# Three down projections as seven products of quadrants for eight, with the sums of quadrants on POOL

## Chip, cores, metric

One of the eight cores of one Trainium2 chip. The metric is the device time of one execution in microseconds, the median over runs.

## The reference

Two transformer blocks of different make over 512 tokens of width 1024; everything is float32. Block one (depth 1) ends with a feed-forward stage of width 4096, block two (depth 2) has in each layer a gated feed-forward stage of width 2816 with a causal convolution over three tokens. Cut to these:

```python
# block one
h2 = rmsnorm(x, norm_ffn_g[l])
x = x + jnp.square(jax.nn.relu(h2 @ w_ff1[l])) @ w_ff2[l]
# block two, in each of two layers
up = u @ w_up
a, g = up[..., :D_FF_2], up[..., D_FF_2:]
a = causal_depthwise_conv(a, conv_w, conv_b)
return (jax.nn.gelu(a, approximate=False) * g) @ w_down
```

`w_ff2` (4096 x 1024) and the two `w_down` (2816 x 1024) are the three down projections.

## The kernel before

Activations lie with features on the 128 partitions and the 512 tokens as columns: `self.x[m]` is feature block m of 8. To keep float32 precision each operand is split into a rounded part and its remainder (`wh`, `wl` for weights, `x.h`, `x.l` for activations) and each product is three matmuls of 512 columns, all three in `lin` (line 503): `wh` x `x.h`, `wl` x `x.h`, `wh` x `x.l`. All matmuls are issued at line 379 (`mm`), all DVE, ACT and POOL instructions at line 221 (a wrapper).

Weights come in chunks of up to 128 x 1024. `fill` (line 426) keeps three chunks in flight on SP's queue (line 432, tile `raw`). ACT copies a chunk into `wh` with rounding (`whi`, line 436), DVE subtracts (`wlo`, line 451) into `wl`. There are four `wh` and three `wl` tiles; `nextw` (line 469) prepares chunks ahead, each time the projection before it has been issued.

`proj` (line 515) runs one output block: takes a PSUM tile, issues the matmuls of its chunks, then spawns its evacuation. In block one (`ffn1`, line 1461) a half of the hidden width is 16 up projections, each evacuated by `hid` (DVE multiplies by the row norm, squares after a comparison with zero, `split` at line 597 makes the two operands with ACT and DVE), then 8 down projections of 16 blocks, added into `self.x[m]` by `xadd` (line 1453). In block two (`ffn2`, line 1813) hidden block m takes two up projections: `conv` (DVE, ACT, DVE twice, ACT for the Gelu) and `gate` (DVE twice, then `split`); 16 blocks, then the down projection over them, then 6 blocks and theirs. In the last part each finished `x[m]` feeds the next norm (`fin1` at line 1502, `feed` at line 610: ACT, DVE, and squares added up on POOL by `sqadd`, line 627).

The order of the instructions on each engine is set when the program is built: generators (the stream of projections, the evacuations) are stepped by `drive` (line 301) in the order of an estimated time. Each engine then takes its own queue strictly in that order, and waits by semaphores.

## Time and profile before

| | |
|---|---|
| median of 3 runs | 2324.68 us (2323.86 to 2325.26) |
| the profiled execution, its own time | 2324.91 us |
| its span, first to last instruction | 2323.2 us |
| mean granted TensorE clock | 0.994 |
| PE, DVE, ACT, POOL busy | 98%, 65%, 46%, 21% of the span |

PE is the matmul engine, DVE the vector engine, ACT the scalar engine, POOL GpSimd, SP the queue that starts transfers. A busy share is an average over stages; which engine holds the others up is told by the waits and by the chain that ended last. Matmuls are pipelined: a row's duration is longer than the distance to the next start, and the distance is what counts in a row of matmuls. "L379" is a line of the kernel before.

### The profile page before, as it was taken

What the parts mean: (1) busy time and instruction counts of PE and PEld (TensorE: products, weight loads), DVE (VectorE), ACT (ScalarE), POOL (GpSimd) and SP (SyncE); (2) the same over time, 40 slices, a digit from 0 to 9 for tenths busy, and PEclk for the clock granted to TensorE, in tenths of its full rate; (3) what the DMA queues carried; (4) which work ended last, traced back from release to release, by engine and by line L of the source; (5) the groups of instructions that cost most, each with busy time, mean ns of one, the idle gap of its engine ahead of it and who ended that gap; (6) DMA issues with size and microseconds to landing.
All of it is one profiled execution on the core that took longest, in us unless ns stands there. A gap on an engine that the chain in (4) does not pass through costs nothing.

```text
span 2323.2 us, 29048 instructions
## 1 busy us (share of the span) xinstructions
PE 2278.9 (98%) x10810; PEld 1868.2 (80%) x10810; DVE 1518.4 (65%) x2375; ACT 1067.4 (46%) x1695; POOL 479.0 (21%) x571
## 2 busy tenths in 40 slices
PE   9999999999999999999999999999999999999998
PEld 6887877778888888887878888888887878888887
DVE  6878499976542554679975652457688866652466
ACT  4767466664322233466643331245556544332343
POOL 3523044431000002334430000002425320000012
PEclk9999999999999999999999999999999999999999
DMA  5321322123332222433333233323432332233332
GB/s 178 87 74 55 91 73 64 56 87 116 98 100 97 94 100 84 155 95 101 119 105 100 93 98 100 102 91 115 125 108 90 118 109 92 99 100 93 107 95 69
DMA packets 75727, 228.24 MB, mean 98 GB/s; under 512 B 9664, under 2 KB 15680, under 8 KB 75584
## 3 DMA queue, kind: packets, MB, share of 16 engines
q1 hardware_dynamic: 70400, 209.62, 28.2%
q0 software_dynamic: 5184, 16.75, 2.5%
q8 instruction: 85, 1.39, 0.3%
q14 instruction: 58, 0.48, 0.1%
HBM read 215.29 MB, written 6.32 MB: 95 GB/s over the span
## 4 chain that ended last, share of the span: by engine, by line
PE 87%; DVE 8%; issue 2%; POOL 1%; ACT 1%; DMA 0%; SPq 0%; POOLq 0%; DVEq 0%; ACTq 0%
PE lin L379 73%; PE v L379 5%; PE sc L379 3%; PE po L379 3%; DVE wl L221 2%; PE pt L389 2%; DVE xl L221 1%; DVE dg L221 1%; DVE eq L221 0%; DVE ks L221 0%; DVE pre L221 0%; DVE qk L221 0%; DVE ql L221 0%; DVE sl L221 0%; DVE suf L221 0%
## 5 line engine op out<-in xcount | busy, mean ns | idle before, releaser
L379 PE MATMUL lin<-xh,wh 128*128 128x512 f32 (+1 forms) x2752 | 1088.0, 395 | 0.0
L379 PE MATMUL lin<-xl,wh 128*128 128x512 f32 (+1 forms) x2752 | 1072.3, 390 | 6.7 <-DVE xl L221 6.7
L379 PE MATMUL lin<-xh,wl 128*128 128x512 f32 (+1 forms) x2728 | 1061.5, 389 | 0.0
L221 DVE TENSOR_TENSOR wl<-raw,wh 128x1024 fp32r<-128x1024 f32 (+3 forms) x391 | 468.9, 1199 | 500.8 <-PE lin L379 329.3
L221 ACT ACTIVATE wh<-raw 128x1024 fp32r<-128x1024 f32 (+4 forms) x394 | 392.4, 996 | 807.7 <-PE lin L379 659.8
L379 PEld LDWEIGHTS lin<-xl,wh 128*128 128x128 f32 x2752 | 517.3, 188 | 117.8 <-DVE xl L221 8.8
L379 PEld LDWEIGHTS lin<-xh,wh 128*128 128x128 f32 x2752 | 518.0, 188 | 105.0 <-issue 3.5
L379 PEld LDWEIGHTS lin<-xh,wl 128*128 128x128 f32 x2728 | 514.4, 189 | 96.7
L221 POOL TENSOR_TENSOR sq<-sq 128x512 f32<-128x512 f32 (+1 forms) x61 | 90.1, 1477 | 566.6 <-ACT sq L221 565.9
L221 POOL MEMSET pad<- 128x2 f32 x44 | 4.4, 99 | 586.3 <-DVE cv L221 586.3
L221 POOL TENSOR_SCALAR P<-P,r 128x128 f32<-128x128 f32 (+3 forms) x128 | 86.5, 681 | 149.3 <-DVE r L221 133.0
L221 DVE SCALAR_TENSOR_TENSOR cv<-pad,vec,cv 128x512 f32<-128x512 f32 x88 | 66.1, 752 | 40.7 <-ACT cv L221 39.0
L379 PE MATMUL v<-wh,xh 128*128 128x512 f32 x192 | 78.3, 408 | 0.7 <-POOL wh L221 0.7
L379 PE MATMUL v<-wl,xh 128*128 128x512 f32 x192 | 75.9, 395 | 3.1 <-DVE wl L221 3.1
L379 PE MATMUL v<-wh,xl 128*128 128x512 f32 x192 | 75.7, 394 | 0.0
L221 ACT ACTIVATE ph<-pt 128x512 fp32r<-128x512 f32 (+3 forms) x128 | 55.6, 435 | 42.2 <-PE pt L389 40.8
L221 DVE TENSOR_TENSOR x<-lin,x 128x512 f32<-128x512 f32 x80 | 54.6, 683 | 23.5 <-PE lin L379 23.5
L221 DVE TENSOR_TENSOR pl<-pt,ph 128x512 fp32r<-128x512 f32 (+3 forms) x128 | 60.2, 479 | 12.7 <-ACT ph L221 12.2
L221 ACT ACT_TABLE_LOAD x51 | 65.4, 1283 | 4.2 <-DVE qk L221 1.6
L221 ACT ACTIVATE P<-lg,m 128x128 f32<-128x128 f32 (+1 forms) x96 | 53.6, 558 | 28.9 <-DVE m L221 21.9
L221 ACT ACTIVATE tl<-po 64x512 f32<-64x512 f32 x56 | 33.2, 592 | 73.1 <-PE po L379 72.6
L221 DVE CUSTOM_DVE_ANT_0 lg<-sc,E 128x128 f32<-128x128 f32 (+1 forms) x96 | 45.6, 483 | 31.9 <-PE sc L379 23.1
(244 smaller groups left out, 2578.1 us busy)
## 6 DMA issues: line engine op xcount, KB each, us to landing
raw<-wup SPq DMA_DIRECT2D x88, 512.0 KB, 3.3
raw<-w SPq DMA_DIRECT2D x83, 512.0 KB, 3.6
raw<-wf SPq DMA_DIRECT2D x64, 512.0 KB, 3.3
raw<-wdn SPq DMA_DIRECT2D x32, 512.0 KB, 3.5
raw<-wv SPq DMA_DIRECT2D x22, 512.0 KB, 3.6
raw<-wpg SPq DMA_DIRECT2D x16, 512.0 KB, 3.3
raw<-wbr SPq DMA_DIRECT2D x12, 512.0 KB, 3.3
raw<-wdn SPq DMA_DIRECT2D x16, 384.0 KB, 3.1
```

What stands on the lines that cost most here:

```text
L221: r = f(*a, **k)
L379: self.nc.tensor.matmul(out, l, r, start=start, stop=stop)
L389: self.nc.tensor.transpose(out, src, self.ident)
```

## The change

Each down projection is cut into blocks of 256 x 256 weights by 256 x 512 activations, as 2 x 2 quadrants on both sides, and the eight quadrant products become seven (Strassen's algorithm in Winograd's form). The inner width goes in parts of four pairs of 128 (block two's last part has three): four parts in block one, three in each layer. `wino` makes two output blocks per call (a quad of weights): seven products, each 3 matmuls of 256 columns for every pair, into three PSUM tiles `wa`, `wg`, `we`; DVE adds partial results straight into the two blocks of `x`, seven additions. Product 3 goes on in the columns that product 0 wrote and its addition has read, product 4 in those of product 1, product 6 in those of 3.

On the weights' side POOL makes four sums of 512 columns per quad (`sums` and `wlo`), in place in the two raw chunks and in a `ws` tile; ACT and DVE then split seven operands. The third sum overwrites the quadrant that the first operand was split from. On the activations' side `hid` and `gate` now write a pair of hidden blocks into one tile, POOL makes four sums of 256 columns per pair and ACT and DVE split seven operands (`bops`). The product of the convolution's result with the row norm, which DVE did from PSUM on the gate, goes to POOL. Squaring goes to ACT. `canhi` and `canlo` prepare weights as soon as a tile's holder has been issued.

```diff
+def _quads(w, pairs):
+    k, m = w.shape
+    assert k == 256 * pairs
+    t = w.reshape(pairs, 2, 128, m // 256, 2, 128).transpose(3, 4, 2, 1, 0, 5)
+    return np.ascontiguousarray(t).reshape(m // 256, 2, 128, 256 * pairs)
...
-    o["wf2"] = _fm(A["w_ff2"][0])
+    o["wf2"] = np.stack([_quads(A["w_ff2"][0][1024 * q:1024 * q + 1024], 4) for q in range(4)])
...
-    o["wdn"] = np.stack([_fm(A["w_down_2"][i], 22)[:, 0] for i in range(2)])
+    o["wdn"] = np.stack([np.stack([_quads(A["w_down_2"][i][1024 * q:1024 * q + 1024], 4) for q in range(2)]) for i in range(2)])
+    o["wdl"] = np.stack([_quads(A["w_down_2"][i][2048:], 3) for i in range(2)])
...
+    def quad(self, ap, n):
+        q = Quad(128 * n, len(self.rawq))
+        for r in range(2):
+            self.rawq.append((ap[r], 256 * n))
+        for k in range(7):
+            self.wq.append((None, 128 * n, 0, q.raw + 1, q, k))
+    def room(self, tag, i):
+        o, n = self.own[tag], self.SLOTS[tag]
+        return len(o) < n or o[-n] < i
+    def canhi(self, i):
+        j = self.wsh
+        q, k = self.wq[j][4:6]
+        if self.wq[j][3] >= self.wdma:
+            return False
+        return self.room("wl" if q and k % 2 else "wh", i)
...
+        if q:
+            src = self.sums(q, k)
+            tag = "wl" if k % 2 else "wh"
+            t = self.ws.tile([128, 2 * cols], F32R, tag=tag, name=tag, bufs=self.SLOTS[tag])
+            self.own[tag].append(j)
+            self.ac.activation(t[:, 0:cols], src, AF.Copy)
+            self.wh[j], self.wl[j] = t[:, 0:cols], t[:, cols:2 * cols]
+            return
...
+    def sums(self, q, k):
+        n = q.n
+        if k == 0:
+            a, b = q.a, q.b = self.raw[q.raw], self.raw[q.raw + 1]
+            assert self.live["tri"] < self.cap["tri"]
+            self.live["tri"] += 1
+            q.t = self.trip.tile([128, 1280], F32, tag="tri", name="ws")
+            self.tags[id(q.t)] = ("tri", q.t)
+            self.pl.tensor_tensor(out=q.t[:, 0:n], in0=b[:, 0:n], in1=b[:, n:2 * n], op=ALU.add)
+            self.pl.tensor_tensor(out=b[:, 0:n], in0=a[:, 0:n], in1=b[:, 0:n], op=ALU.subtract)
+        return (q.a[:, 0:n], q.t[:, 0:n], q.a[:, n:2 * n], q.a[:, 0:n], q.t[:, 512:512 + n], q.b[:, n:2 * n], q.b[:, 0:n])[k]
...
+        if q:
+            self.dv.tensor_tensor(out=self.wl[j], in0=self.sums(q, k) if k else q.a[:, 0:q.n], in1=self.wh[j].bitcast(F32),
+                                  op=ALU.subtract)
+            n = q.n
+            if k == 0:
+                self.pl.tensor_tensor(out=q.a[:, 0:n], in0=q.t[:, 0:n], in1=q.a[:, 0:n], op=ALU.subtract)
+                self.pl.tensor_tensor(out=q.t[:, 512:512 + n], in0=q.a[:, n:2 * n], in1=q.a[:, 0:n], op=ALU.subtract)
+            if k == 4:
+                self.free(q.t)
+                self.raw.pop(q.raw)
+                self.rawdone += 1
+                self.fill()
+            if k == 6:
+                self.raw.pop(q.raw + 1)
+                self.rawdone += 1
+                self.fill()
+            return
...
-        while self.wsh < min(n, i + 4):
+        while self.wsh < n and self.canhi(i):
             self.whi()
-            while self.wsl < min(self.wsh - 1, i + 3):
+            while self.wsl < self.wsh - 1 and self.canlo(i):
                 self.wlo()
-        while self.wsl < min(n, i + 3, self.wsh):
+        while self.wsl < self.wsh and self.canlo(i):
             self.wlo()
...
+    def bops(self, pr):
+        h = S // 2
+        b11, b12, b21, b22 = (pr.t[:, h * j:h * j + h] for j in range(4))
+        def split(k, src):
+            o = pr.ops[k]
+            o.h = yield from self.g("bo", F32R)
+            self.ac.activation(o.h[:, 0:h], src, AF.Copy)
+            yield self.w("ac")
+            self.dv.tensor_tensor(out=o.h[:, h:S], in0=src, in1=o.h[:, 0:h].bitcast(F32), op=ALU.subtract)
+            self.sig(o.ev, "dv")
+        yield pr.e[0]
+        yield from self.take("tw", 1, 3)
+        T = yield from self.tri("T")
+        t1, t2, t3, t4 = (T[:, h * j:h * j + h] for j in range(4))
+        self.pl.tensor_tensor(out=t1, in0=b12, in1=b11, op=ALU.subtract)
+        yield from split(0, b11)
+        yield from split(1, t1)
+        yield pr.e[1]
+        self.pl.tensor_tensor(out=t2, in0=b22, in1=t1, op=ALU.subtract)
+        self.pl.tensor_tensor(out=t4, in0=b21, in1=t2, op=ALU.subtract)
+        self.pl.tensor_tensor(out=t3, in0=b22, in1=b12, op=ALU.subtract)
+        yield from split(2, b21)
+        yield from split(4, b22)
+        yield from split(3, t2)
+        yield from split(5, t4)
+        yield from split(6, t3)
+        yield self.w("dv")
+        self.free(pr.t, T)
+        self.give("tw", 2)
+    def btile(self, pr):
+        if pr.t is None:
+            yield from self.take("tw", 1, 3)
+            pr.t = yield from self.tri("bt")
+            self.spawn(self.bops(pr), 1)
+    def wino(self, ap, n, prs, m, done):
+        self.quad(ap, n)
+        h = S // 2
+        def run():
+            x1, x2 = self.x[m], self.x[m + 1]
+            def prod(k, o, start):
+                wh, wl = self.nextw()
+                for i in range(n):
+                    b = prs()[i].ops[k]
+                    yield from self.need(b)
+                    c = slice(128 * i, 128 * i + 128)
+                    self.mm(o, wh[:, c], b.h[:, 0:h], start and i == 0, False, True)
+                    self.mm(o, wl[:, c], b.h[:, 0:h], False, False, True)
+                    self.mm(o, wh[:, c], b.h[:, h:S], False, i == n - 1, True)
+                    yield None
+            def add(x, p):
+                self.dv.tensor_tensor(out=x, in0=p, in1=x, op=ALU.add)
+            a = yield from self.psr("lin", self.lincap, "wa")
+            yield from prod(0, a[:, 0:h], True)
+            add(x1[:, 0:h], a[:, 0:h])
+            g = yield from self.psr("lin", self.lincap, "wg")
+            yield from prod(1, g[:, 0:h], True)
+            add(x2[:, h:S], g[:, 0:h])
+            e = yield from self.psr("lin", self.lincap, "we")
+            yield from prod(2, e[:, 0:h], True)
+            yield from prod(3, a[:, 0:h], False)
+            add(x1[:, h:S], a[:, 0:h])
+            yield from prod(4, g[:, 0:h], False)
+            add(x1[:, h:S], g[:, 0:h])
+            self.free(g)
+            yield from prod(5, e[:, h:S], False)
+            add(x1[:, 0:h], e[:, 0:h])
+            add(x2[:, 0:h], e[:, h:S])
+            self.free(e)
+            yield from prod(6, a[:, 0:h], False)
+            u = a[:, 0:h]
+            add(x2.rearrange("p (a c) -> p a c", a=2), bass.AP(u.tensor, u.offset, [list(u.ap[0]), [0, 2], [1, h]]))
+            self.free(a)
+            if done:
+                for j in range(2):
+                    self.spawn(self.later(done, m + j), 0)
+        self.tasks.append(run)
...
-        def hid(X_):
+        def hid(pr, e):
             def run(ps):
-                nc = self.nc
-                t = yield from self.g("h")
+                yield from self.btile(pr)
+                t = pr.t[:, S * e:S * e + S]
                 yield N2.ev
-                self.dve_mul(t, ps, N2.rb)
+                self.dv.scalar_tensor_tensor(out=t, in0=ps, scalar=0.0, in1=N2.rb, op0=ALU.max, op1=ALU.mult)
                 self.free(ps)
-                self.dv.scalar_tensor_tensor(out=t, in0=t, scalar=0.0, in1=t, op0=ALU.max, op1=ALU.mult)
                 yield self.w("dv")
-                yield from self.split(t, X_)
+                self.ac.activation(t, t, AF.Square)
+                self.sig(pr.e[e], "ac")
             return run
 
         N = Norm()
         N1 = Norm()
-        for half in range(2):
-            hs = [X() for _ in range(16)]
-            for m in range(16):
-                self.proj([(I["wf1"][16 * half + m], 1024)], lambda: N2.xs, hid(hs[m]))
-            if half:
+        for part in range(4):
+            prs = [Pair() for _ in range(4)]
+            for m in range(8):
+                self.proj([(I["wf1"][8 * part + m], 1024)], lambda: N2.xs, hid(prs[m // 2], m % 2))
+            if part == 3:
                 self.call(lambda: self.nfree(N2))
-            nxt = (lambda m: self.fin1(N1, N, m)) if half else None
-            for m in range(KT):
-                self.proj([(I["wf2"][m, 2 * half + g], 1024) for g in range(2)], lambda hs=hs: hs,
-                          lambda ps, m=m, nxt=nxt: self.xadd(m, ps, nxt))
-            self.call(lambda hs=hs: [self.free(x.h, x.l) for x in hs])
+            nxt = (lambda m: self.fin1(N1, N, m)) if part == 3 else None
+            for j in range(4):
+                self.wino(I["wf2"][part, j], 4, lambda prs=prs: prs, 2 * j, nxt)
+            self.call(lambda prs=prs: [self.free(o.h) for pr in prs for o in pr.ops])
...
                 self.ac.activation(c, c, AF.Gelu)
+                yield self.w("ac")
+                self.pl.tensor_tensor(out=c, in0=c, in1=N.rb, op=ALU.mult)
                 cx.h = c
-                self.sig(cx.ev, "ac")
+                self.sig(cx.ev, "gp")
             return run
 
-        def gate(cx, X_):
+        def gate(cx, pr, e):
             def run(ps):
-                nc = self.nc
-                t = yield from self.g("gt")
-                yield N.ev
-                self.dve_mul(t, ps, N.rb)
-                self.free(ps)
+                yield from self.btile(pr)
                 yield cx.ev
-                self.dv.tensor_tensor(out=t, in0=t, in1=cx.h, op=ALU.mult)
-                self.free(cx.h)
-                yield self.w("dv")
-                yield from self.split(t, X_)
+                self.dv.tensor_tensor(out=pr.t[:, S * e:S * e + S], in0=ps, in1=cx.h, op=ALU.mult)
+                self.free(ps, cx.h)
+                self.sig(pr.e[e], "dv")
             return run
 
-        for part, (lo, hi) in enumerate(((0, 16), (16, nf))):
-            hs = [X() for _ in range(hi - lo)]
-            for m in range(lo, hi):
+        for part, n in enumerate((4, 4, 3)):
+            prs = [Pair() for _ in range(n)]
+            for j in range(2 * n):
+                m = 8 * part + j
                 cx = X()
                 self.proj([(I["wup"][i, m], 1024)], lambda: N.xs, conv(m, cx))
-                self.proj([(I["wup"][i, nf + m], 1024)], lambda: N.xs, gate(cx, hs[m - lo]))
-            if part:
+                self.proj([(I["wup"][i, nf + m], 1024)], lambda: N.xs, gate(cx, prs[j // 2], j % 2))
+            if part == 2:
                 self.call(lambda: self.nfree(N))
                 self.ple_proj(i, 1, pp)
-            cuts = ((0, 8), (8, 16)) if part == 0 else ((16, 22),)
-            nxt = (lambda m: self.feed(N3, m, self.x[m], f"ple{i}")) if part else None
-            for m in range(KT):
-                self.proj([(I["wdn"][i, m][:, 128 * a:128 * b], 128 * (b - a)) for a, b in cuts], lambda hs=hs: hs,
-                          lambda ps, m=m, nxt=nxt: self.xadd(m, ps, nxt))
-            self.call(lambda hs=hs: [self.free(x.h, x.l) for x in hs])
+            nxt = (lambda m: self.feed(N3, m, self.x[m], f"ple{i}")) if part == 2 else None
+            for j in range(4):
+                w = I["wdn"][i, part, j] if part < 2 else I["wdl"][i, j]
+                self.wino(w, n, lambda prs=prs: prs, 2 * j, nxt)
+            self.call(lambda prs=prs: [self.free(o.h) for pr in prs for o in pr.ops])
```

The order on the engines moves with it. First DVE, in block one where the first part of the hidden width is done and the down projections begin (`h` and `bt` are evacuated hidden activations, `wl` and the halves of `wh` and `wl` that DVE writes are weight remainders, `bo` activation operands, `wa`, `wg`, `we` the accumulators of a quad). Before:

```order
L221 TENSOR_TENSOR wl<-raw,wh 128x1024 [waits DMAHW0_49,PE_49]
L221 TENSOR_TENSOR h<-lin,rb 128x512 [waits PE_49]
L221 SCALAR_TENSOR_TENSOR h<-h 128x512 [waits DVE_49]
L221 TENSOR_TENSOR xl<-h,xh 128x512 [waits Activation_49]
L221 TENSOR_TENSOR wl<-raw,wh 128x1024 [waits DMAHW1_49,PE_49]
L221 TENSOR_TENSOR wl<-raw,wh 128x1024 [waits DMAHW2_49,PE_49,Activation_49]
L221 TENSOR_TENSOR x<-lin,x 128x512 [waits PE_49]
```

With the change:

```order
L231 TENSOR_TENSOR wl<-raw,wl 128x512 [waits DMAHW7_49,DVE_49,Activation_49]
L231 TENSOR_TENSOR wh<-raw,wh 128x512 [waits Activation_49]
L231 SCALAR_TENSOR_TENSOR bt<-lin,rb 128x512
L231 TENSOR_TENSOR x<-wa,x 128x256 [waits PE_49]
L231 TENSOR_TENSOR wh<-raw,wh 128x512 [waits DMAHW0_49,DVE_49,Activation_49]
L231 TENSOR_TENSOR x<-wg,x 128x256 [waits PE_49]
L231 TENSOR_TENSOR wl<-ws,wl 128x512 [waits Activation_49]
L231 TENSOR_TENSOR bo<-bt,bo 128x256 [waits Activation_49] x2
L231 TENSOR_TENSOR wh<-raw,wh 128x512 [waits Activation_49]
L231 TENSOR_TENSOR bo<-T,bo 128x256 [waits Pool_49]
```

Two weight subtractions now stand ahead of the last evacuation (`bt<-lin,rb`); the first subtraction of the next quad follows the addition of product 0 (`x<-wa,x`), and the last pair's operands (`bo<-bt,bo`, `bo<-T,bo`) come after that.

Second POOL, in block two's first layer at the same crossing (`pad` and `cv` belong to the convolution, `ws` and `raw` to a quad's weight sums, `T` to a pair's sums). Before, at the same place, eighteen repeats in one row:

```order
L221 TENSOR_TENSOR rt<-ms,cst 128x4 [waits DVE_49]
L221 MEMSET pad 128x2
L221 MEMSET pad 128x2 [waits DVE_49,Activation_49,Pool_49] x18
L221 DMA p<-pT 128x512 [waits DMASW2_49,PE_49]
L221 DMA p<-pT 128x512 [waits DMASW3_49,PE_49]
```

With the change:

```order
L231 TENSOR_TENSOR T<-bt 128x256 [waits DVE_49]
L231 MEMSET pad 128x2
L231 TENSOR_TENSOR ws<-raw 128x512 [waits DMAHW1_49]
L231 TENSOR_TENSOR raw<-raw 128x512 [waits DMAHW0_49,DVE_49,Pool_49]
L231 TENSOR_TENSOR raw<-ws,raw 128x512 [waits DMAHW2_49,DMAHW5_49,DVE_49,Pool_49]
L231 TENSOR_TENSOR ws<-raw 128x512 [waits Pool_49]
L231 TENSOR_TENSOR cv<-cv,rb 128x512 [waits PE_49]
L231 TENSOR_TENSOR T<-bt,T 128x256 [waits DVE_49]
L231 TENSOR_TENSOR T<-bt,T 128x256 [waits Pool_49]
L231 TENSOR_TENSOR T<-bt 128x256
```

The four weight sums of the second quad stand ahead of the last convolution's product with the norm (`cv<-cv,rb`), which stands ahead of the last pair's sums.

## Rows read from the trace of the kernel before

**Rows 1.** The page's first part: busy us, share, instructions.
```profile
PE 2278.9 (98%) x10810; PEld 1868.2 (80%) x10810; DVE 1518.4 (65%) x2375; ACT 1067.4 (46%) x1695; POOL 479.0 (21%) x571
```

**Rows 2.** Chain that ended last, block one's feed-forward stage: start us, us, what.
```profile
597.86 342.76 PE lin L379 x1512
```

**Rows 3.** PE's timeline, last projection: start us, us, instruction (first, last of 86).
```profile
2299.54 0.28 PE L379 MATMUL lin<-xh,wl 128*128 128x256 f32 x1
...
2309.74 0.28 PE L379 MATMUL lin<-xl,wh 128*128 128x256 f32 x1
```

**Rows 4.** Groups by line and form: xcount, busy us, mean ns, idle before, releaser.
```profile
L379 PEld LDWEIGHTS lin<-xh,wh 128*128 128x128 f32 x2736 | 515.8, 189 | 103.8 <-issue 3.5
L221 DVE TENSOR_TENSOR wl<-raw,wh 128x1024 fp32r<-128x1024 f32 x329 | 418.1, 1271 | 447.9 <-PE lin L379 293.8 <-issue 126.6 <-PE v L379 24.3
L221 DVE TENSOR_TENSOR xl<-h,xh 128x512 fp32r<-128x512 f32 x32 | 22.1, 692 | 20.6 <-ACT xh L221 20.5
L221 DVE TENSOR_TENSOR x<-lin,x 128x512 f32<-128x512 f32 x80 | 54.6, 683 | 23.5 <-PE lin L379 23.5
L221 DVE TENSOR_TENSOR st<-sc,dec 128x256 f32<-128x256 f32 x16 | 6.5, 408 | 0.0
L221 DVE TENSOR_TENSOR pl<-pt,ph 128x384 fp32r<-128x384 f32 x32 | 17.4, 544 | 2.3 <-ACT ph L221 2.2
L221 DVE SCALAR_TENSOR_TENSOR xl<-x,vec,xh 128x512 fp32r<-128x512 f32 x56 | 53.8, 975 | 3.9 <-ACT xh L221 3.6
L221 DVE TENSOR_SCALAR x<-x,vec 128x512 f32<-128x512 f32 x8 | 5.0, 626 | 4.9 <-ACT sq L221 4.9
L221 ACT ACTIVATE wh<-raw 128x512 fp32r<-128x512 f32 x25 | 15.7, 628 | 17.2 <-PE lin L379 15.4 <-ACT sg L221 1.6
L221 ACT ACTIVATE ph<-pt 128x256 fp32r<-128x256 f32 x32 | 12.2, 381 | 9.9 <-PE pt L389 9.5
```

**Rows 5.** Timeline of POOL: one product of 512 columns by itself.
```profile
317.47 1.28 POOL L221 TENSOR_TENSOR ek<-k,ek 128x512 f32<-128x512 f32 x1 [1.54 <-ACT ek L221]
```

**Rows 6.** Timeline of POOL and DVE at 876 and at 1202 us.
```profile
876.62 2.26 POOL L221 TENSOR_TENSOR sq<-sq 128x512 f32<-128x512 f32 x1 [1.64 <-ACT sq L221]
876.50 1.23 DVE L221 TENSOR_TENSOR wl<-raw,wh 128x1024 fp32r<-128x1024 f32 x1 [1.24 <-PE lin L379]
877.65 1.78 DVE L221 SCALAR_TENSOR_TENSOR xl<-x,vec,xh 128x512 fp32r<-128x512 f32 x1
...
1201.82 7.18 POOL L221 TENSOR_TENSOR sq<-sq 128x512 f32<-128x512 f32 x4 [0.84 <-ACT sq L221]
1202.12 2.31 DVE L221 TENSOR_TENSOR wl<-raw,wh 128x1024 fp32r<-128x1024 f32 x1
1204.35 0.68 DVE L221 TENSOR_TENSOR x<-lin,x 128x512 f32<-128x512 f32 x1
1204.95 2.90 DVE L221 SCALAR_TENSOR_TENSOR xl<-x,vec,xh 128x512 fp32r<-128x512 f32 x2
```

**Rows 7.** DVE's timeline, block one's first crossing, up to down projections.
```profile
675.23 1.23 DVE L221 TENSOR_TENSOR wl<-raw,wh 128x1024 fp32r<-128x1024 f32 x1 [1.50 <-PE lin L379]
...
678.48 0.69 DVE L221 TENSOR_TENSOR xl<-h,xh 128x512 fp32r<-128x512 f32 x1 [0.70 <-ACT xh L221]
```

**Rows 8.** PE's timeline at 1211 us; in brackets idle time, releaser.
```profile
1211.40 0.50 PE L379 MATMUL lin<-xl,wh 128*128 128x512 f32 x1 [0.90 <-DVE xl L221]
...
1214.81 0.79 PE L379 MATMUL lin<-xl,wh 128*128 128x512 f32 x1 [2.44 <-DVE xl L221]
```

**Rows 9.** Two stretches: busy us (instructions) by engine, granted clock, DMA.
```profile
core 0: us, PE busy (x) PEld busy (x) DVE busy (x) ACT busy (x) POOL busy (x), PEclk, DMA share, GB/s
1200.00:1210.00 10.00, 10.00 (x46) 8.29 (x45) 10.00 (x8) 8.16 (x12) 7.93 (x5) 1.00 0.32 105
1210.00:1220.00 10.00, 6.66 (x25) 4.77 (x24) 8.68 (x12) 3.55 (x5) 2.24 (x3) 0.83 0.32 105
```

**Rows 10.** The page's DMA issues: xcount, KB each, us to landing.
```profile
raw<-wdn SPq DMA_DIRECT2D x32, 512.0 KB, 3.5
```

71 lines of the change are left out of this document (49 added, 22 removed).

## Prediction

> **What bounds the kernel now.** Read the busy table first [rows 1]: PE has work in 98% of the span, DVE in 65%, POOL in 21%. So time is won only by taking work from PE's queue, and lost only where PE starts to wait. A busy share does not tell whether PE runs at its best rate, so the chain that ended last comes second, over the first block's feed-forward stage: one unbroken piece of 1512 matmuls in 342.76 us [rows 2]. That gives 0.2267 us from one start to the next for 512 columns, and it says that in this stage, which crosses from up to down projections twice, PE waits for nobody. Third, the matmuls of half that width: the last projection already has them, 86 starts in a row, each with its own weights, 10.20 us for 85 steps [rows 3], so 0.120 us each. Half the columns cost 53% of the time, not 50%; this decides what seven products for eight can give.
>
> **What is removed from PE and added.** The down projections are 32 x 8 x 3 = 768 matmuls in block one and 22 x 8 x 3 = 528 in each layer of block two, 1824 of 512 columns: 1824 x 0.2267 = 413.5 us. Four of these become seven products of 256 columns, so 3192 x 0.120 = 383.0 us. **Term 1: -30.4 us**, on the path, as PE is. Bounds: without the fixed part of a matmul it would be an eighth, -51.7 us; the row of the very same form is taken without reserve.
> The Trainium skill ("TensorE: Matmul & The Clock Gate", section "Back-to-back issue gap") gives columns / 2.4 plus about 2.5 ns. By it the two widths would cost 215.8 and 109.2 ns and the gain would be an estimated 45 us; the trace disagrees at both widths (226.7 and 120.0 ns), so its rows decide.
>
> **What DVE, ACT and POOL get.** I call the eight products' replacement for two output blocks a quad: 40 quads, ten runs of four. A quad of four pairs is 84 matmuls, 10.08 us. For it ACT copies 7 x 0.628 = 4.4 us. DVE has seven subtractions of 512 (0.692), six additions of 256 from PSUM (like the 0.408 row) and one of 512 (0.683): 7.98 us [rows 4]; before, the same share was two subtractions of 1.27 and one addition's worth, 3.2 us. POOL has four sums, S1 to S4, of 512: 1.28 each when undisturbed [rows 5], 5.12 us. All fit under 10.08 singly. The evacuation that goes away (one DVE pass of 0.69 per up projection) lies beside PE and pays nothing. Two-operand DVE instructions from SBUF and POOL's sums do not run side by side, though: at 876.62 a POOL sum of 1.28 takes 2.26 because a DVE subtraction began before it, and the next DVE instruction then takes 1.78 where its form's mean is 0.98; at 1202 four POOL sums and the DVE instructions between them take strict turns, and an addition from PSUM (0.68) is not held up [rows 6]. So 4.84 + 5.12 = 9.96 us per quad share one resource that PE outruns in 10.08.
>
> **The crossings from up to down.** The old cover: the last evacuation's subtraction ended at 679.17, about 4 us after PE let go of that projection [rows 7], and its operand was first needed 15 x 3 x 0.2267 = 10.2 us in. The new cover: the last pair's third operand is needed by the third matmul of pair four in product 2, at 24 x 0.12 + 9 x 0.12 + 0.24 = 4.2 us after the last up projection (call that time zero), its fourth at 5.6 us. What is queued in front is what the order on DVE and POOL shows.
> In block two (four crossings into runs of four pairs) the last convolution's multiply by the row norm is new on POOL and stands behind S1 to S4 of the second quad. S3 overwrites what DVE's first subtraction of that quad reads, and that stands behind the addition of product 0. So: product 0 ends 1.44, addition 0.41, subtraction 0.69, S3 and S4 2.56, the multiply 1.28, DVE's gate 0.68, ACT's copy 0.38, DVE's subtraction 0.41: 7.85 us, needed at 4.2. Stall 3.7 at least. Two subtractions of the first quad stand before that addition and meet S1 and S2, and S3 and S4 meet another: up to 0.7 + 3 x 1.28 later, about 8 us. I take 6.5, nearer the turns of rows 6.
> In block one (four crossings) three have two subtractions and then the evacuation in front of the addition. They wait for weight slots that PE frees at time zero: 2.3, evacuation 0.69, addition 0.41, subtraction 0.69, S3 and S4 2.56, the pair's sum of 256 on POOL 0.65 (half of 1.28), copy 0.38, subtraction 0.41: 8.1, needed at 5.6: at least 2.5, with the turns up to 6.5; I take 5. In the fourth the evacuation comes first: 1 to 4, taken 3. The two crossings into runs of three pairs have 24 matmuls of another projection between (5.4 us) and cost nothing.
> **Term 2: 4 x 6.5 + 3 x 5 + 3 = +44 us**, from 23 to 55.
>
> **The clock.** After idle times of 0.90 and 2.44 us [rows 8] the granted clock falls to half, so that 1210 to 1220 shows 0.83: 1.7 us lost [rows 9]. Eight crossings with such gaps: 0 to 13.6, **term 3: +8 us**.
>
> **Inside the runs.** A POOL sum that starts behind a subtraction holds the next one up by up to 1.28 - 0.41, four times a quad: 7.98 + 3.5 = 11.5 us against 10.08. PE notices when an addition is over 2.9 us late (product 3 writes again into what product 0's addition reads, two products later). Only two quads of a run carry such sums beside them. 0 to 10 us over seven runs, **term 4: +4 us**. The weights' own loop (transfer 3.5 us [rows 10], S1 to S4, copy, subtraction: 3.5 + 5.12 + 0.63 + 0.69 = 9.9 us a quad, perhaps 2 more with the turns) may be slower than PE, but its first transfer starts before time zero, a whole quad early, and a run has only three such steps: nothing.
> The last run of each stage also feeds the next norm. Block one: DVE 7.98 + 2 x (0.975 + 0.626) = 11.2 us a quad, and with the squares' sums on POOL some 16.5 on the shared resource against 10.08; block two with three pairs: 7 x 0.544 + 2.45 + 0.68 + 1.95 = 8.9 against 7.56, shared 11.7. Two quads each, less the 2.9 of slack: 0 to 20 together, **term 5: +13 us**.
>
> **Sum**: -30.4 + 44 + 8 + 4 + 13 = +38.6. The profiled execution took 2324.91 us (span 2323.2), 0.2 over the median of 2324.68; so **2364 us**. All low ends give 2318, all high ones 2393. About 0.2%, 4.6 us, is what a measurement here can tell from no change.
>
> **Rivals.**
> *The cover holds (faster).* If the third quad-weight transfer lands early and S1 to S4 of the second quad are done before time zero, the crossings cost under 1 us each, and 2294 plus about 10 for clock and last runs gives 2297 to 2312. For it: PE never waited here before [rows 2]. Against: S3 needs a subtraction that stands behind product 0 in DVE's own order. The point that decides: 3 us a crossing eats the gain. 0.13.
> *Only the fixed order counts.* No turns, no fallen clock: crossings 23 to 30, 2318 to 2330. Against: rows 6 and 9. 0.14.
> *DVE and POOL's shared resource sets the pace throughout.* Each quad with sums beside it goes at 11.5 us or more, the crossings at their high ends, 2390 to 2420. For it: 9.96 of 10.08 is full, and at 1200 to 1210 the same two engines, DVE 10.00 busy and POOL 7.93, held PE up [rows 8, 9]. The Trainium skill ("SBUF — State Buffer", section "SBUF: two separate sides") has it as a lock held for a whole instruction, against which nothing but waiting helps; the trace agrees (2.26 us for 1.28). 0.18.
> *Half-width matmuls wait for their weights.* The load row's mean is 189 ns [rows 4]; if that bound, 3192 x 0.189 = 603 us, +190, about 2515. Against: rows 3, every matmul there has new weights. 0.02.
>
> **How the numbers follow.** The forecast (2335 to 2390) keeps 0.53. Slower: 0.53 + 0.18 + 0.02, and 0.02 of the fixed-order case: 0.75. Within 0.2%: 0.09 of that case. Faster: 0.13 + 0.03: 0.16. The range runs from 2310, which leaves out most of the covered case, to 2400.
>
> **What would show it.** Right: 3192 matmuls of 256 columns 0.120 us apart; PE idle before the third and fourth products at eight crossings, released by DVE's operand subtractions, behind POOL's multiply in block two; clock dips after them; POOL sums of over 1.28 us and DVE subtractions of over 0.69 in the runs. Wrong: gapless crossings, or matmuls at another distance; or idle time in the middle of runs that exceeds that at the crossings.

## The result, and the profile after

The change makes the kernel slower: 2411.16 us (2410.52 to 2413.30) against 2324.97 us, a ratio of 1.0373 with an interval of 1.0355 to 1.0390. The profiled execution has a span of 2409.5 us at a mean granted clock of 0.979, against 2323.2 us at 0.994. The forecast was 2364, its range ended at 2400: the sign was right, the size was not.

The page's first part, after, beside [rows 1]:

```profile
PE 2281.0 (95%) x12178; PEld 1929.1 (80%) x12178; DVE 1835.1 (76%) x2921; ACT 1210.6 (50%) x2117; POOL 904.7 (38%) x927
```

POOL's work nearly doubled and PE's share fell from 98% to 95%, though PE was given less to do. Inside the runs of seven products PE does what [rows 3] promised. The chain that ended last, in the middle of block one's first run (start us, us, what), answers to [rows 2]:

```profile
656.59 2.88 PE wa L391 x24
659.47 1.44 PE wg L391 x12
660.91 1.44 PE we L391 x12
...
666.67 2.88 PE wa L391 x24
```

Twelve matmuls of 256 columns in 1.44 us are 0.120 each, and a quad comes every 10.08 us (656.59, 666.67) without a gap. The loss is at the edges. PE's timeline where block two's first run begins:

```profile
1335.86 1.60 PE L391 MATMUL wa<-bo,wh 128*128 128x256 f32 x12
1337.29 1.60 PE L391 MATMUL wg<-bo,wl 128*128 128x256 f32 x12
1338.73 1.24 PE L391 MATMUL we<-bo,wh 128*128 128x256 f32 x9
1347.46 1.22 PE L391 MATMUL we<-bo,wh 128*128 128x256 f32 x3 [7.49 <-ACT bo L231]
```

Nine of product 2's twelve matmuls run; then PE waits 7.5 us for the third operand of the last pair. Block one's first run has the same place, with two waits:

```profile
636.99 0.80 PE L391 MATMUL we<-bo,wh 128*128 128x256 f32 x2 [3.39 <-ACT bo L231]
639.78 0.58 PE L391 MATMUL we<-bo,wh 128*128 128x256 f32 x1 [1.99 <-DVE bo L231]
```

POOL and DVE at block two's crossing:

```profile
1337.87 1.86 POOL L231 TENSOR_TENSOR ws<-raw 128x512 f32<-128x512 f32 x1 [4.44 <-DMA raw<-wdn]
1339.81 1.59 POOL L231 TENSOR_TENSOR raw<-raw 128x512 f32<-128x512 f32 x1
1342.08 1.26 POOL L231 TENSOR_TENSOR raw<-ws,raw 128x512 f32<-128x512 f32 x1 [0.68 <-DVE wh L231]
1343.42 1.59 POOL L231 TENSOR_TENSOR ws<-raw 128x512 f32<-128x512 f32 x1
1344.97 1.26 POOL L231 TENSOR_TENSOR cv<-cv,rb 128x512 f32<-128x512 f32 x1
...
1338.48 1.79 DVE L231 TENSOR_TENSOR wh<-raw,wh 128x512 fp32r<-128x512 f32 x1
1340.20 0.41 DVE L231 TENSOR_TENSOR x<-wa,x 128x256 f32<-128x256 f32 x1
1340.53 1.42 DVE L231 TENSOR_TENSOR wh<-raw,wh 128x512 fp32r<-128x512 f32 x1
...
1346.26 0.69 DVE L231 TENSOR_TENSOR bt<-lin,cv 128x512 f32<-128x512 f32 x1 [2.37 <-POOL cv L231]
```

This is the chain of the prediction: S1 to S4, the multiply, the gate. Subtractions of 0.69 take 1.42 to 1.79 beside POOL's sums, the addition from PSUM keeps its 0.41. One thing the prediction had not counted stands in the first row: S1 waits for a transfer. At all eight crossings into runs of four pairs the second quad's second chunk lands 1.6 to 2.2 us after the last up projection, and S1 and S2 then run beside the first quad's two subtractions; the addition of product 0, which stands behind those, starts 4.3 us after the last up projection here (1340.20) instead of the forecast's 1.44, and 5.3 to 6.1 in block one, where the forecast's chain gave 3.0.

The clock, in the middle of block one's first run and behind block two's wait (start and end, length, busy us and count of PE, PEld, DVE, ACT, POOL, granted clock, DMA share, GB/s):

```profile
646.51:656.59 10.08, 10.08 (x86) 10.08 (x86) 9.96 (x13) 4.42 (x7) 5.84 (x4) 1.00 0.28 94
1347.00:1352.00 5.00, 4.54 (x20) 4.41 (x21) 3.26 (x6) 3.00 (x7) 2.39 (x3) 0.50 0.00 0
```

In the first stretch PE has no gap although DVE is busy for 9.96 of 10.08 us. In the second, after the idle time, PE is granted 0.50, the lower level (1.2 of 2.4 GHz). The last parts, PE's timeline in block two's first layer (three pairs, nine matmuls a product):

```profile
1598.70 0.38 PE L391 MATMUL we<-bo,wh 128*128 128x256 f32 x1 [0.53 <-DVE bo L231]
...
1602.99 0.58 PE L391 MATMUL wa<-bo,wl 128*128 128x256 f32 x1 [2.74 <-DVE bo L231]
...
1616.24 2.38 PE L391 MATMUL wa<-bo,wh 128*128 128x256 f32 x18 [1.68 <-DVE x L231]
...
1627.26 2.39 PE L391 MATMUL wa<-bo,wh 128*128 128x256 f32 x18 [2.15 <-DVE x L231]
```

One number for each run makes kernels comparable: **the loss of a run**, from its first matmul to the first one behind it, less its matmuls x 0.120 us (336, in the three-pair runs 252). It holds idle time and slow clock alike. Each run has four quads; where only the first one loses, the loss belongs to the crossing. In the changed kernel:

| runs | loss of each, us | together |
|---|---|---|
| block one, first three | 8.4, 8.2, 8.2 | 24.8 |
| block one, fourth (feeds the next norm) | 16.7 | 16.7 |
| block two, four pairs | 10.6, 10.0, 10.1, 9.7 | 40.4 |
| block two, three pairs (feed the next norm) | 11.7, 11.6 | 23.3 |
| all ten | | 105.1 |

The gain of 30.4 less these 105.1 makes +74.7 of the +86.3 in span; 11.6 lie outside the runs. In seven of the runs all of the loss is in the first quad. In block one's fourth run the first quad loses 7.7 and the later ones 9.0; in the two runs of three pairs it is 10.7 and 12.5 together.

### The profile page after: what moved, and what is told of

It is laid out like the page before. It is cut to its first block, busy times and chain, and to the rows that moved or that the text cites. A ratio compares the mean times of both kernels' runs of the same rounds, so it can differ in the third digit from the quotient of the medians.

```text
span 2409.5 us, 33516 instructions
## 1 busy us (share of the span) xinstructions
PE 2281.0 (95%) x12178; PEld 1929.1 (80%) x12178; DVE 1835.1 (76%) x2921; ACT 1210.6 (50%) x2117; POOL 904.7 (38%) x927
## 4 chain that ended last, share of the span: by engine, by line
PE 72%; DVE 16%; POOL 4%; issue 4%; ACT 2%; DMA 1%; SPq 0%; POOLq 0%; DVEq 0%; ACTq 0%
PE lin L391 47%; PE v L391 6%; PE wa L391 5%; PE we L391 3%; PE wg L391 3%; PE sc L391 3%; DVE wh L231 3%; DVE wl L231 3%; PE po L391 2%; DVE xl L231 2%; DVE x L231 1%; PE pt L401 1%; POOL ws L231 1%; POOL raw L231 1%; POOL T L231 1%
## 5 line engine op out<-in xcount | busy, mean ns | idle before, releaser
L391 PE MATMUL lin<-xh,wh 128*128 128x512 f32 (+2 forms) x2144 | 852.0, 397 | 1.0 <-DVE st L231 0.5
L391 PE MATMUL lin<-xl,wh 128*128 128x512 f32 (+2 forms) x2144 | 835.7, 390 | 9.3 <-DVE xl L231 9.2
L391 PE MATMUL lin<-xh,wl 128*128 128x512 f32 (+1 forms) x2120 | 824.9, 389 | 0.0
L231 ACT ACTIVATE wh<-raw 128x1024 fp32r<-128x1024 f32 (+3 forms) x434 | 383.1, 883 | 531.1 <-PE lin L391 275.3
L231 DVE TENSOR_TENSOR wl<-raw,wh 128x1024 fp32r<-128x1024 f32 (+2 forms) x311 | 379.6, 1221 | 234.2 <-PE lin L391 148.1
L391 PEld LDWEIGHTS lin<-xl,wh 128*128 128x128 f32 (+1 forms) x2144 | 402.9, 188 | 98.6 <-DVE xl L231 12.7
L391 PEld LDWEIGHTS lin<-xh,wh 128*128 128x128 f32 (+1 forms) x2144 | 403.6, 188 | 82.1 <-issue 3.5
L231 DVE TENSOR_TENSOR wh<-raw,wh 128x512 fp32r<-128x512 f32 (+2 forms) x123 | 145.9, 1186 | 5.9 <-ACT wh L231 5.5
L391 PE MATMUL wa<-bo,wh 128*128 128x256 f32 x912 | 119.3, 285 | 13.2 <-DVE x L231 13.2
L391 PEld LDWEIGHTS wa<-bo,wh 128*128 128x128 f32 x912 | 114.8, 194 | 15.2 <-issue 8.3
```

Source lines behind the costliest of these rows:

```text
L231: r = f(*a, **k)
L391: self.nc.tensor.matmul(out, l, r, start=start, stop=stop, skip_group_check=skip)
```

## The experiments

Three theories: **order** (a block of four sums stands in front of urgent work in a fixed queue), **turns** (DVE's two-operand instructions and POOL's sums exclude each other), **load** (the two engines simply have too much to do). The expectations call order "theory A" and the shared resource, turns and load together, "theory B". Times are medians where there are several runs; e1 to e7, e13 and e17 ran once.

**1. The price of the weight sums.** `e3_no_wsums` drops them.

```diff
-            self.pl.tensor_tensor(out=q.t[:, 0:n], in0=b[:, 0:n], in1=b[:, n:2 * n], op=ALU.add)
-            self.pl.tensor_tensor(out=b[:, 0:n], in0=a[:, 0:n], in1=b[:, 0:n], op=ALU.subtract)
...
-                self.pl.tensor_tensor(out=q.a[:, 0:n], in0=q.t[:, 0:n], in1=q.a[:, 0:n], op=ALU.subtract)
-                self.pl.tensor_tensor(out=q.t[:, 512:512 + n], in0=q.a[:, n:2 * n], in1=q.a[:, 0:n], op=ALU.subtract)
```

> The four weight sums of each quad (S1 to S4) are left out: the seven operands are split from plain quadrants; all else, DVE's and ACT's passes and all matmuls, stays. The price of POOL's weight sums altogether, order and turns. Theory A: crossings as with the sums held back (about 2 in block two, 1.6 in block one), 2365 or a little less, and the last runs of each stage (32 us lost beyond their crossings in the changed kernel) keep most of their loss, as DVE's own 11.2 and 8.9 us a quad pace them: 2350 to 2368. Theory B: the last runs recover too, since without POOL's sums DVE's passes take their plain 0.69: 2325 to 2345.

Measured 2341.29, in theory B's range; loss in the runs 35.4 instead of 105.1. The sums alone are worth 70 us, as much as all the losses of the forecast together (69). The last pair of product 2 is now 1.4 and 2.1 us late, near theory A's 1.6 and 2; the last runs lose 6.9 and 4.0 (from 16.7 and 11.6), so they recover too, against what theory A said of them. Order and turns go away together here, so this run does not tell them apart. And even without the sums the kernel stays 16 us above the one before: 35.4 of loss is more than the 30.4 gained.

**2. Order at the crossings.** `e1_hold` and `e5_hold_late` keep the second quad's weights back until product 3 or product 6 (`j - 4`, `j - 1`).

```diff
+        if q and q.held and k == 0 and i < j - 4:
+            return False
```

> Only the second quad's weights are held back: its first operand, and so its four weight sums on POOL, is prepared no earlier than product 3 of the first quad. Changed kernel: PE idle 7.86 us per crossing in block two (four), 6.4 in block one (three) and 5.7 at the fourth, and with the low clock behind them about 73 us. Theory A (the fixed order: what stands in front of the last pair's work on POOL and DVE costs the crossing): in block two cv, the gate, the copy and the subtraction remain, so third operand at about 6 us after the last up projection against 3.8 needed: stall about 2; block one about 1.6. Time about 2411 - 4 x 6.5 - 3 x 5.5 - 3 = 2365 (2355 to 2380). Theory B (DVE and POOL share a resource that is full, so a delay moves with the sums): the stall turns up again after product 3 or in the second quad; time 2395 to 2415.

Measured 2418.79. That is above both ranges. The first wait fell as theory A said, and a longer one stood one product later. PE, then DVE, in block one's first run:

```profile
633.83 0.51 PE L391 MATMUL we<-bo,wh 128*128 128x256 f32 x2 [0.83 <-ACT bo L231]
...
642.65 0.58 PE L391 MATMUL wa<-bo,wl 128*128 128x256 f32 x1 [6.42 <-DVE bo L231]
...
638.32 1.20 DVE L231 TENSOR_TENSOR wl<-ws,wl 128x512 fp32r<-128x512 f32 x1 [1.81 <-ACT wl L231]
639.45 1.75 DVE L231 TENSOR_TENSOR wh<-raw,wh 128x512 fp32r<-128x512 f32 x1
641.12 2.15 DVE L231 TENSOR_TENSOR bo<-T,bo 128x256 fp32r<-128x256 f32 x3
```

The last pair's fourth operand (`bo<-T`) now stands behind the second quad's subtractions, which wait for POOL's sums. Order decides where the wait is.

> As the first hold, but the second quad's weights wait until product 6 of the first quad, when all of the last pair's operands have been issued. In the first hold the stall before product 2's last pair fell from 6.4 to 1.2 us, and 6.8 us came back one product later, because the second quad's subtractions (waiting for POOL's sums) now stood ahead of the last pair's fourth operand on DVE. Theory A (order): both places short, 1 to 2.5 us a crossing; but the second quad's own chain (sum 1.3, copy 0.6, subtraction 0.7 per operand, third sum behind a subtraction) now starts only 1.4 us before its first product and may stall it by 1 to 3: 2411 - 8 x (9 - 2 - 2.5 - 1) = about 2383 (2365 to 2395). Theory B (the sums' time on the shared resource has to be paid wherever they stand next to a crossing): 6 to 8 us come back at the second quad's products 1 to 3, 2405 to 2420.

Measured 2397.09, between the two. The first quads of the eight crossings lose 18.8 us instead of 72.9, but the quads behind them lose 52.3 instead of 9.0, first with a wait of 2.6 us for an addition in the second quad. The sums have to fit somewhere.

`e2_cv_back` undoes one part: DVE multiplies the gate by the norm again, POOL no longer the convolution's result.

```diff
-                self.pl.tensor_tensor(out=c, in0=c, in1=N.rb, op=ALU.mult)
...
+                self.dve_mul(t, ps, N.rb)
...
+                self.dv.tensor_tensor(out=t, in0=t, in1=cx.h, op=ALU.mult)
```

> Only one part of the change is undone: the multiply by the row norm goes back from POOL (on the convolution's result) to DVE (on the gate, out of PSUM). Weight sums stay where they are. If POOL's fixed order is what costs block two's crossings, the last gate no longer waits for S1 to S4 (it ended at 1346.23, the convolution's result was there at 1338.63): stall 7.9 -> 3 to 6 (S3, S4 still in front of the pair's own sums), time 2411 - 4 x (2 to 5) = 2391 to 2403, block one unchanged. If the shared resource decides, one more DVE pass per hidden block brings nothing or a loss: 2408 to 2420.

Measured 2403.34, at the end of theory A's range: loss of block two's four runs 40.4 to 29.3, block one's first three unchanged (25.6).

`e13_spread_sums_only` places S1 with operand 1, S2 and S3 with operand 3, S4 with operand 4, still on POOL.

> The changed kernel with this one edit: S1 to S4 stay on POOL and keep their number and length, but are spread over operands 1, 3 and 4 of their quad instead of standing in a block with its first operand. Order theory: at a crossing S3 and S4 of the second quad no longer stand ahead of the convolution's multiply and the last pair's sums, and only one sum instead of four meets the last pair's subtractions: the stalls fall from 6.4 and 7.9 us to 2 to 4, the last runs lose less than now: 2411 - 7 x 5 - 10 = 2366 (2350 to 2385). Load theory (DVE and POOL cannot do more in the time, wherever the sums stand): 2400 to 2415.

Measured 2408.78; loss 103.8. That is the range of the load theory. Taken by itself, this order is worth next to nothing: block two's four runs lose 34.9 instead of 40.4, but block one's lose 46.1 instead of 41.5, with new waits at the run's first product (0.93 for ACT's copy, 0.26 for DVE's operand).

**3. Turns at the crossings.** `e4_dve_wsums` makes the sums on DVE (`self.pl` to `self.dv` in the four lines), `e17_changed_sums_dve_spread` also spreads them, one operand ahead of use: S1 with operand 0, S2 and S3 with 2, S4 with 3.

> S1 to S4 are made by DVE instead of POOL (0.69 each instead of 1.28 and no turns between the engines; DVE gets 2.8 us more per quad, 10.7 against PE's 10.08 in a quad that prepares the next one). If the turns with POOL set the crossings: stalls fall to 3 to 4 in each, 2375 to 2395, last runs of the stages a little better or the same. If only the order counts (the sums still stand in front of the last pair's work, now on DVE): block two falls to about 7.85 - 4 x 0.6 = 5.5, block one to about 5, 2390 to 2400. If DVE's load decides: stalls in the middle of the runs, above 2411.

> The changed kernel itself, with nothing but the sums on DVE and one operand ahead: crossings uncovered, seven products in the last parts, new look-ahead. With the same sums in a block on DVE it took 2399, crossings late by 4.3 (block one) and 4.8 to 5.1 (block two). If the block in front is what made the crossings late, what stays is the conv's own chain, as without any sums (1.4 and 2.0): about 3 less at eight crossings and less low clock, 2399 - 8 x 4 = 2367, and the last runs some 5 less: 2350 to 2372. If it is not the block: 2385 to 2400.

Measured 2398.75 and 2382.25, losses 85.6 and 74.8. Without turns, with as much in front, PE still waits 4.4 to 4.7 us in product 2 of a crossing (3.0 at block one's fourth); spreading takes 16 us more. 2382 lies between the two ranges: the three-pair runs stay at 12.5 and 14.9.

The first quads of the eight crossings compare the theories:

| kernel | sums | loss of the eight first quads, us |
|---|---|---|
| changed | POOL, block | 72.9 |
| e13 | POOL, spread, at use | 72.4 |
| e4 | DVE, block | 53.7 |
| e17 | DVE, spread, one ahead | 40.9 |
| e3 | none | 21.7 |

Taking the sums off POOL gives 19 back, spreading them gives 13 more once they are off POOL: order and turns each hold a part of a crossing, and 22 stay without any weight sums. (POOL's sums one operand ahead were not tried in this kernel, nor an earlier transfer for S1, so the transfer's share is open.)

**4. Cover.** `e6_ups_ahead` issues the first two up projections of the next part ahead of each run; `e7_last_eight` gives the three last parts eight products; `e8_ahead_and_last_eight` does both.

```diff
+                if m == 1:
+                    tail()
...
-            for j in range(4):
-                self.wino(I["wf2"][part, j], 4, lambda prs=prs: prs, 2 * j, nxt)
...
+            def tail(part=part, prs=prs, nxt=nxt):
+                for j in range(4):
+                    self.wino(I["wf2"][part, j], 4, lambda: prs, 2 * j, nxt)
```

> The first two up projections of the next part are issued before each run of seven products (where the stage has a next part: three of block one's four crossings, all four long ones of block two), 10.9 us of matmuls between the last pair's projections and the run. Nothing else changes. Theory A: third and fourth operands are late by 6.4 and 7.9 us in the changed kernel, so 10.9 us cover both: no stall and no low clock at seven crossings, 3 x 8.3 + 4 x 10.1 = 65 us less: 2346 (2343 to 2356); the last runs unchanged. Theory B: the runs now carry a pair's evacuation beside the sums, DVE and POOL fall behind PE, and stalls of several us appear inside the runs: 2370 or more.

> The last part of each stage (the fourth of block one, the third of either layer of block two) goes back to eight products of 512 columns with two operands per block; the seven other parts stay. If the last runs lose because DVE and POOL carry the next norm beside sums and partial additions: the changed kernel's last runs take 57.0, 42.0 and 41.8 us; as eight products 192 x 0.2267 = 43.5 and 144 x 0.2267 = 32.6 twice, plus 0 to 2 at each crossing: 30 us less, and 4 to 7 less behind them, as the last block of x is ready earlier: 2376 (2370 to 2384). If the loss belongs to the norm's own work and not to the seven products, 2395 or more.

> Both of the two edits before: up projections ahead of seven runs of seven products, and eight products in the three last parts. If the two causes are separate, their gains add: 2411 - 65 - 35 = 2311 (2304 to 2322), faster than the kernel before (2325), since seven runs each save 43.5 - 40.3 = 3.2 us, 22.5 together, with nothing given back. If the runs themselves cost time next to other work, 2330 or more.

Measured 2389.50, 2374.20 and 2344.48 (ratio to before 1.0085, 1.0068 to 1.0102). Only e7 came out as expected: in the last parts PE no longer waits. e6 and e8 missed their gains (2346 and 2311). The cover removed every late operand in the seven runs, but they kept 34 us of loss, all of it in waits for additions and the slow clock. PE, DVE and POOL of the third kernel:

```profile
1325.61 1.66 PE L392 MATMUL wa<-bo,wl 128*128 128x256 f32 x12 [1.22 <-DVE x L232]
...
1320.97 2.96 DVE L232 TENSOR_TENSOR bo<-T,bo 128x256 fp32r<-128x256 f32 x2
1323.85 0.68 DVE L232 TENSOR_TENSOR wl<-raw,wl 128x512 fp32r<-128x512 f32 x1
1324.45 0.68 DVE L232 TENSOR_TENSOR wh<-raw,wh 128x512 fp32r<-128x512 f32 x1
1325.05 0.41 DVE L232 TENSOR_TENSOR x<-wa,x 128x256 f32<-128x256 f32 x1
...
1320.48 1.73 POOL L232 TENSOR_TENSOR ws<-raw 128x512 f32<-128x512 f32 x1 [3.03 <-DMA raw<-wdn]
1322.29 1.36 POOL L232 TENSOR_TENSOR raw<-raw 128x512 f32<-128x512 f32 x1
```

Two subtractions of 0.41 take 2.96 beside two sums, and the addition that product 3 needs stands behind them.

**5. The look-ahead rule.** `e11_before_new_lookahead` is the kernel before with nothing but the new rule for when weights are prepared; `e9_ahead_last_eight_dve_wsums` is the last kernel with sums on DVE, `e10_e9_old_lookahead` the same with the old rule for ordinary chunks.

```diff
-        while self.wsh < min(n, i + 4):
+        while self.wsh < n and self.wsh < self.wdma and self.room("wh", i):
```

> The kernel before, with only the new rule for when weights are prepared (as soon as the tile's holder has been issued). If the rule costs the attention stages: 2325 + 4 to 10 = 2329 to 2335. If the extra time there came from the products' own side effects: 2325 within 2 us.

> The kernel with up projections ahead of the runs and eight products in the last parts (2344), and S1 to S4 now on DVE. In that kernel no operand is late any more, but in every run PE still waits 2 to 5 us for the additions into x, because DVE's operand subtractions take 1.5 us instead of 0.4 while POOL makes weight sums, and the additions stand behind them on DVE. If the turns between the two engines are what is left: DVE gets 2.8 us more per quad but loses no turns; stalls in the runs fall from 34 us in all to under 10: 2344 - 25 = 2319 (2312 to 2328), below the kernel before. If DVE's sheer load is what is left (10.7 us a quad and a pair's evacuation in the same run, against 10.08), 2344 or more.

> The same, and for ordinary chunks of weights the old rule again (hi parts at most four items ahead, lo parts three), which the change replaced for all weights; items of quads keep the new one. The changed kernel and its variants spend about 6 and 3 us more in the two attention stages behind a feed-forward stage than the kernel before, where nothing else differs. If that rule is the cause: 6 to 10 us less than the run before it. If not: within 2 us of it.

Measured 2330.61 (1.0027, 1.0016 to 1.0039), 2340.27 and 2335.89. The rule costs 6 us without any Strassen in the kernel, 5 of them between block one's feed-forward stage and block two's first; the reversal gives 4 back in the median (the intervals of e9, 1.0052 to 1.0086, and e10, 1.0028 to 1.0058, overlap). e9 and e10 came out between their forecasts. Moving the sums to DVE won little (loss 29.7 and 31.9, from 34.1): the block now stands on DVE, ahead of the addition of product 1. DVE, then PE, of the third:

```profile
643.87 0.69 DVE L232 TENSOR_TENSOR ws<-raw 128x512 f32<-128x512 f32 x1
...
648.01 0.69 DVE L232 TENSOR_TENSOR ws<-raw 128x512 f32<-128x512 f32 x1
648.62 0.42 DVE L232 TENSOR_TENSOR x<-wg,x 128x256 f32<-128x256 f32 x1
...
649.09 2.93 PE L392 MATMUL wg<-bo,wh 128*128 128x256 f32 x12 [2.42 <-DVE x L232]
```

**6. Order, turns or load, with the crossings out of the way.** All on `e10`: `e12_e10_spread_sums` spreads as in 2, `e15_sums_one_operand_ahead` as in 3, `e16_sums_after_second_addition` keeps the block and moves it behind that addition, `e18_e15_sums_on_pool` is `e15` with POOL making the sums. From e10 to e15:

```diff
+            if k == 2:
+                self.dv.tensor_tensor(out=b[:, 0:n], in0=a[:, 0:n], in1=b[:, 0:n], op=ALU.subtract)
+                self.dv.tensor_tensor(out=a[:, 0:n], in0=q.t[:, 0:n], in1=a[:, 0:n], op=ALU.subtract)
+            if k == 3:
+                self.dv.tensor_tensor(out=q.t[:, 512:512 + n], in0=a[:, n:2 * n], in1=a[:, 0:n], op=ALU.subtract)
...
-            if k == 0:
-                self.dv.tensor_tensor(out=q.a[:, 0:n], in0=q.t[:, 0:n], in1=q.a[:, 0:n], op=ALU.subtract)
-                self.dv.tensor_tensor(out=q.t[:, 512:512 + n], in0=q.a[:, n:2 * n], in1=q.a[:, 0:n], op=ALU.subtract)
```

> The run before it (2336: up projections ahead, eight products last, sums on DVE, old look-ahead), but the four sums of a quad are no longer issued together with its first operand: S1 stands with operand 1, S2 and S3 with operand 3, S4 with operand 4. There, PE's 32 us of loss in the seven runs come from additions into x that stand on DVE behind a block of four sums (in the trace five instructions, 643.9 to 648.6, ahead of the addition that PE waits for). If the block is the cause: stalls under 1 us a run, 2336 - 25 = 2311 (2305 to 2318), 0.5% below the kernel before. If DVE's load in the run is the cause (the same instructions, only spread): 2330 or more.

> As the kernel with up projections ahead, eight products last, sums on DVE and the old look-ahead (2336), the sums spread, but each one operand earlier than in the spread that failed: S1 with operand 0, S2 and S3 with operand 2, S4 with operand 3. There DVE stood idle 0.76 three times a quad, between a sum and the subtraction directly behind it, for ACT's copy of that sum (10.7 + 2.3 = 13 us a quad against 10.08). If that round trip is what spoiled it: no such idle time, additions at most 1 us late: 2310 to 2322. If DVE's load is the limit anyway: 2330 to 2350.

> The same kernel of 2336, sums in one block on DVE, but the block starts one product later, behind the addition of product 1 instead of in front of it. In 2336 PE waits up to 2.8 us in every run for just that addition; the next addition in the queue is product 3's, which is needed 2.9 us later than the block ends. If it is only the place of the block: 32 us of loss in the runs fall to 5 to 10, 2310 to 2317. If DVE's load decides: the wait moves to product 6, 2330 or more.

> The fastest version so far (2309: up projections ahead, eight products last, old look-ahead, sums one operand ahead on DVE), with the sums back on POOL, in the same places. It prices the turns between the engines by themselves. If turns matter only where a block of sums stands in front of something urgent: within 5 us of 2309. If they hold DVE up whenever a sum runs (1.3 us four times a quad): 2325 to 2345, additions late in every run.

| run | us | ratio to before (interval) | loss in seven runs |
|---|---|---|---|
| e10 (block) | 2335.89 | 1.0043 (1.0028 to 1.0058) | 31.9 |
| e12 (spread, at use) | 2352.41 | 1.0116 (1.0101 to 1.0131) | 51.3 |
| e16 (block, later) | 2319.25 | 0.9976 (0.9965 to 0.9987) | 17.2 |
| e15 (spread, one ahead) | 2308.62 | 0.9926 (0.9911 to 0.9941) | 3.7 |
| e18 (as e15, on POOL) | 2338.03 | 1.0064 (1.0047 to 1.0080) | 33.3 |

The losses are those of the profiled executions; e10's took 2328.85, its other three about 2336. e16 fell between its forecasts (17.2 of loss instead of 5 to 10). The miss, e12, has a new wait: a sum, ACT's copy of it and the subtraction directly behind it on DVE, three times a quad (DVE of e12):

```profile
647.21 0.89 DVE L232 TENSOR_TENSOR ws<-raw 128x512 f32<-128x512 f32 x1
648.86 0.69 DVE L232 TENSOR_TENSOR wl<-ws,wl 128x512 fp32r<-128x512 f32 x1 [0.76 <-ACT wl L232]
```

One operand earlier, with the same instructions, five of the seven runs lose under 0.2 us and two 1.7 each: load was not the limit. The chain of e15, in block two's first run, has a quad every 10.08 us again:

```profile
1325.83 2.88 PE wa L392 x24
...
1335.91 2.88 PE wa L392 x24
```

e18 repeats that order with turns; the addition that PE waits for stands behind stretched subtractions. PE and DVE of e18:

```profile
1327.29 1.70 PE L392 MATMUL wa<-bo,wl 128*128 128x256 f32 x12 [2.08 <-DVE x L232]
...
1321.30 4.39 DVE L232 TENSOR_TENSOR bo<-T,bo 128x256 fp32r<-128x256 f32 x3
...
1326.82 0.41 DVE L232 TENSOR_TENSOR x<-wa,x 128x256 f32<-128x256 f32 x1
```

The groups by line and form, of e15, then of e18:

```profile
L232 DVE TENSOR_TENSOR wh<-raw,wh 128x512 fp32r<-128x512 f32 x85 | 59.0, 695 | 0.0
L232 DVE TENSOR_TENSOR wl<-ws,wl 128x512 fp32r<-128x512 f32 x28 | 19.5, 695 | 2.1 <-ACT wl L232 1.9
```

```profile
L232 DVE TENSOR_TENSOR wh<-raw,wh 128x512 fp32r<-128x512 f32 x85 | 99.6, 1172 | 0.4 <-ACT wh L232 0.2
L232 DVE TENSOR_TENSOR wl<-ws,wl 128x512 fp32r<-128x512 f32 x28 | 35.2, 1259 | 7.7 <-ACT wl L232 7.7
```

The same subtraction takes 695 ns or 1172 ns, and the seven runs lose 3.7 or 33.3 us. DVE's idle time for ACT's copy in front of `wl<-ws` grows too, from 2.1 to 7.7 us: 29.6 us is the price of the sums on POOL with everything that follows from it, of which the turns are the part seen in the durations. (`e14_e12_sums_on_pool`, e12's order on POOL, took 2350.97, with a loss of 46.4 against e12's 51.3. e12's round trip is in its path, so this pair does not price the turns by themselves.) e15 is 0.74% faster than the kernel before. Its seven runs save 7 x (192 x 0.2267 - 40.32) = 22.4 us and give 3.7 back, -18.7 in all; measured -16. It is not the change as such: seven of ten runs have seven products, under cover, with the sums on DVE and the old look-ahead for ordinary chunks.

## Why the prediction was wrong

- **Term 1 (-30.4) was right.** 0.120 us from start to start, 10.08 a quad; 53% of a 512-column matmul, not 50%.
- **Terms 2 and 3 (+44, +8) named the right chain and sized it too low.** Measured 73 for the eight crossings: from start to start, 55 in steps of over 0.3 us more than 0.120, the late operands, and 18 in the rest, the slow clock. In block two they are 7.6 us late instead of 6.5, in block one 6.2 to 6.3 instead of 5, and 5.5 at the fourth instead of 3 (its range ended at 4). The step that failed is "I take 6.5, nearer the turns of rows 6": the high end of 8 was nearer, because S1 and S2 met both subtractions ahead of product 0's addition. That they did has a reason the prediction put at "nothing", the weights' own loop: its first transfer came early as said, but the one that S1 waits for landed 1.6 to 2.2 us after time zero. For the clock the row at hand, 1.7 lost after idle times of 0.90 and 2.44 us [rows 8, 9], was discounted to 1; behind these crossings 1.9 to 3.0 were lost.
- **Term 4 (+4) was 0.** The middle quads of the seven runs are gapless; what DVE lost there in turns must have stayed within the slack of 2.9 us.
- **Term 5 (+13, at most 20): 32 measured, in two parts.** "The two crossings into runs of three pairs ... cost nothing" was false: their first quads lose 10.7, with waits of 0.53 and 2.74 and slow clock, because DVE takes the last pair's operands only in the run, behind the quad's subtractions. The later quads of the three last runs, what the term was for, lose 21.5 (9.0 in block one's fourth, 12.5 in the two of three pairs), mostly before additions into `x`. Its shared sums, "some 16.5" and 11.7, show no working and cannot be had again from the rows. e3 puts most of the 40 us in these three runs on the weight sums (15 left without them); e7 shows that with eight products none of it is left.
- **Missing altogether:** the look-ahead rule (+6 in the kernel before, shown by e11) and the rest outside the runs (11.6 - 6, cause open). The diff's rule was read as a detail of the quads, but it acts on all weights.
- **The rivals.** The time came out in the bracket of "DVE and POOL's shared resource sets the pace throughout" (2390 to 2420), with the crossings near their high ends as it said, but not by its mechanism: that it hit the number is luck, as runs do not go at 11.5 us a quad. The prediction's own signs of being right were seen (only that ACT's copy and not DVE's subtraction ended the long wait in block two), and none of its signs of being wrong; beside the steps above it was the sizes that failed. The resource counts where the order puts a block of sums in front of something urgent.

The sum: -30.4 + 73 + 32 + 11.6 = +86.2, against +86.3 in span and a forecast of +38.6. Of the 48 between, 21 are in terms 2 and 3, 11 in the three-pair crossings, 8 in the rest of term 5, 12 outside the runs; term 4 takes 4 off.

## What to carry to other kernels

Where a change puts new work on an engine with spare time, price it at the edges of a stage, not by busy shares: in the changed kernel 5.1 us of sums per quad were free in the middle of seven runs and cost 70 us in all, at the crossings and in the last runs. Where two engines take turns on a resource, take the high end of the wait for every instruction that is queued ahead of a due one, ask when the transfers that feed them land, and count the slow clock behind each idle time in full. Place such work one step ahead of its use, off the engine that shares, and with other matmuls between it and the switch of stage: then seven products for eight paid in seven of ten runs (2308.62 us, 16 below the kernel before).
